# Recurrent gates as three products of split halves, with low parts made ahead, in a two-layer flow-matching step on one Trainium2 core

## The chip, the cores and the metric

The kernel runs on one core of one Trainium2 chip. The metric is the device time of one execution in microseconds (us). Before the change the median of three runs is 1498.4 us (1496.66 to 1498.74).

## The reference, cut to what matters

Two layers run over 512 latent and 128 context tokens of width 1024. Layer 0 mixes tokens by attention, layer 1 by a bidirectional gated linear recurrence; each is followed by a SwiGLU feed-forward of hidden width 2816, and each sub-layer is normed and modulated by vectors computed from a conditioning vector (`silu(cond) @ w_mod + b_mod`). What the change touches is the recurrence:

```python
gate, xr = jnp.split(xm @ w_in, 2, axis=-1)
xc = _centred_depthwise_conv(xr, conv_w, conv_b)
# for each direction, in 8 blocks of 128 channels:
r = jax.nn.sigmoid(jnp.einsum('btnk,nkj->btnj', xb, w_a) + b_a)
i = jax.nn.sigmoid(jnp.einsum('btnk,nkj->btnj', xb, w_i) + b_i)
log_a = -LRU_C * r * jax.nn.softplus(-lam)
a = jnp.exp(log_a)
b = jnp.sqrt(-jnp.expm1(2.0 * log_a)) * (i * xc)
h = a_t * h + b_t                      # scan over the tokens
y = (hs_f + hs_b) * jax.nn.gelu(gate)
return y @ w_out
```

So each block of 128 channels has four gate matrices of 128 x 128: two kinds (w_a, w_i) by two directions.

## The kernel before, in words

Activations lie with channels on the 128 partitions and tokens along the free axis; KT = 8 tiles of 128 channels, 640 tokens. Nearly all matrix products are done in a fast four-byte type (F32R) that rounds its operands. To keep the precision, every operand is split into a high part (a rounded copy) and a low part (the rest), and a product is three: high by high, high by low, low by high (`some`, L232 to 241). A weight is fetched by `unit` (L170): SP loads the raw weight (`raw`, three buffers), then either ScalarE copies it into the rounded type (L186) or, in phases whose only PSUM tag is "at" or where the call asks for it, POOL's queue loads it a second time with a cast (L184); VectorE subtracts to give the low part (L188). High and low parts have three buffers each (`whi`, `wlo`), with another set (`whx`, `wlx`) in some phases.

A weight unit of the feed-forward is eight k-tiles by three products by two chunks of tokens (322 and 320 columns: the first has two extra columns that carry the shift). `ffn` (L994) takes the hidden tiles in three groups of 8, 7 and 7: gate and up units of a group, then its down projection. In the first feed-forward five PSUM banks (three of `mm`, two of `mx`) take the chunks in turn, and VectorE and ScalarE empty them.

The modulation vectors are not matrix products on TensorE: they are sums on VectorE (`mod_cols`, L260), one 512 KB tile of w_mod at a time through POOL's queue into `mraw` (two buffers), with `mprod` (one buffer) for the product that nobody reads. They are written as a generator, 80 steps in all. `fill(n)` (L295) takes n steps of it out of a quota at set places in the program: after each weight unit's fetch and each down tile (FG = 1, 1, 1 says how many, for gate and up units and down tiles). `need` takes as many as it must.

The first feed-forward ends in `project_closing` (L657 on): the last down projection, the statistics and, in `normed`, the modulated norm of the recurrent layer's input, on VectorE and ScalarE in turns (L614 to 616), while TensorE already starts on the first input weights of the recurrent layer.

The recurrent layer goes over eight blocks f, software-pipelined by the loop at L1629: `lru_a(t)` convolves the block's input (one ScalarE step, L1395, and three on VectorE, L1397) and computes the four gate products (L1407) and their tanh (L1408); `lru_xr(t+1)` projects the next block's input; `lru_b(t-1)` makes a and b; `lru_c(t-2)` scans; `lru_gate` projects the gelu branch, `lru_d` multiplies and splits the output. Both projections take their weights through `halves` and `unit` (16 tiles of `wi`). The gate products are in single precision: gw (256 KB a block, loaded by SP, L1393) and xc are plain F32, the 643 columns (512 latent, 3 of padding, 128 context) are done as 512 and 131 in a two-bank PSUM tile `gp` with two buffers. The last block ends in `lru_end`, and `project_halves` goes on with the output weights (`wlo`), whose first parts of the product run before the last block is done (L1093, L1097).

The order of instructions on each engine is not the program's: a scheduler places them, by its own model of their times, with the program's order as priority; `pin` and `issue_after` add an order by hand. Each engine then runs its list in order.

Of the kernel before, what the change touches and what calls it, by code (L numbers as in the profile page):

```python
# [9 lines left out]
F32 = mybir.dt.float32  # L10
F32R = mybir.dt.float32r
AF = mybir.ActivationFunctionType
# [3 lines left out]
P = 128  # L16
# [15 lines left out]
EPS = 1e-6  # L32
NEG = -1e30
VW = 256
LW = 643
NLT = 10
C0 = 515
LATPR = (slice(0, 512), slice(C0, LW))
FG = (1, 1, 1)
MODS = ((0, 2), (0, 4), (0, 3), (0, 5), (1, 1), (1, 0), (1, 4), (1, 3), (1, 2), (1, 5))  # L40
NB = 2
KH = KT // 2
# [85 lines left out]
class _Step:  # L128
# [38 lines left out]
        self.read = self.nc.sync.dma_start(t, src).ins  # L167
        return t

    def unit(self, src, slot=None, after=None, nx=3, cast=False, raw=None):  # L170
        nc = self.nc
        _, a, b = src.shape
        raw = self.raw(src) if raw is None else raw
        if slot is None:
            self.nu += 1
            slot = "x" if self.wx and self.nu % 2 == 0 else "m"
        if slot == "x":
            hi, lo = self.wxs([P, a, b], nx)
        else:
            hi = self.t([P, a, b], F32R, "whi", 3)  # L180
            lo = self.t([P, a, b], F32R, "wlo", 3)
        if cast or self.ptags == ["at"]:
            with self.pin(self.cast if after else None):
                nc.gpsimd.dma_start(hi, src)  # L184
        else:
            nc.scalar.copy(hi, raw)  # L186
        with self.pin(after):
            self.low = nc.vector.tensor_tensor(lo, raw, hi.bitcast(F32), ALU.subtract).ins  # L188
        return hi, lo
# [96 lines left out]
    def modulations(self):  # L286
        yield from self.mod_gate(0, 2)
        yield from self.mod_ss(0, 3, 1)
        yield from self.mod_gate(0, 5)
        yield from self.mod_ss(1, 0, 0)  # L290
        yield from self.mod_ss(1, 3, 1)
        yield from self.mod_gate(1, 2)
        yield from self.mod_gate(1, 5)

    def fill(self, n):  # L295
        for _ in range(min(n, self.quota)):
# [697 lines left out]
    def ffn(self, l, hi, lo, fp, last):  # L994
        nc = self.nc
        f0 = 0
        for ci, n in enumerate((8, 7, 7)):
            hhi = self.big()
            hlo = self.big()
            sg = {}  # L1000

            def eg(j):
                def ev(t0, s, ps):
                    if t0:
                        sg[j] = self.t([P, NTOK], F32, "sg", 2, fp)
                    g = sg[j]
                    nc.vector.tensor_tensor(g[:, s], ps, self.rt[:, s], ALU.mult)
                    for c, a, b in _pieces(s.start, s.stop):
                        nc.scalar.activation(g[:, a:b], g[:, a:b], AF.Silu, bias=self.bias[:, c:c + 1])
                return ev  # L1010

            def eu(j):
                def ev(t0, s, ps):
                    u = self.t([P, 320], F32, "up", 2, fp)
                    nc.vector.tensor_tensor(u, ps, self.rt[:, s], ALU.mult)
                    for c, a, b in _pieces(s.start, s.stop):
                        g = sg[j][:, a:b]
                        nc.vector.scalar_tensor_tensor(g, u[:, a - t0:b - t0], self.bias[:, c:c + 1], g, ALU.add, ALU.mult)
                    self.split(hhi[:, j, s], hlo[:, j, s], sg[j][:, s])
                return ev  # L1020
            for j in range(n):
                f = f0 + j
                self.ws(self.i["gu"][l, f], hi, lo, eg(j), FG[0] * (f > 0), CHB)
                self.ws(self.i["gu"][l, NF + f], hi, lo, eu(j), FG[1] * (f > 0), CHB)
            w = self.i["dn"][l, :, :, f0:f0 + n]
            if ci == 2:
                last(w, hhi, hlo, (l, 5))
            else:
                self.project(w, hhi, hlo, (l, 5), done=lambda f: self.fill(FG[2]))
            f0 += n  # L1030
# [332 lines left out]
        c = CI["ba0"] * KT  # L1363
        nc.vector.tensor_scalar(self.hb, self.cols[:, c:c + 4 * KT], 0.5, None, ALU.mult)

    def halves(self, w, hi, lo, ev, after=None, slot=None):
        u = self.unit(w, slot, after, 2)
        return [lambda t0=t0, t1=t1, **kw: ev(t0, self.chunk(u, hi, lo, t0, t1, **kw)) for t0, t1 in CHL]

    def lru_xr(self, f, hi, lo, after=None):  # L1370
        xr = self.xrs[f % 2]
        nat = xr[:, 2:514].rearrange("p (r c) -> p c r", r=ROWS)

        def ev(t0, ps):
            for o, a, b, r in ((nat[:, 56:64], 0, 64, ROWS), (nat[:, 0:40], 64, 384, ROWS),
                               (nat[:, 40:56], 384, 512, ROWS), (xr[:, 517:645], 512, 640, 0)):
                if t0 <= a and b <= t0 + 384:
                    v = ps[:, a - t0:b - t0]
                    self.nc.scalar.copy(o, v.rearrange("p (c r) -> p c r", r=r) if r else v)
        return self.halves(self.i["wi"][KT + f], hi, lo, ev, after)  # L1380

    def turn(self, table, step):
        if table != self.table:
# [5 lines left out]

    def lru_a(self, f, lp):  # L1390
        nc, xr = self.nc, self.xrs[f % 2]
        gw = self.t([P, 2, 2, P], F32, "gw", 2, lp)
        nc.sync.dma_start(gw, self.i["wg"][f])  # L1393
        xc = self.t([P, LW], F32, "xc", 2, lp)
        nc.scalar.activation(xc, xr[:, 0:LW], AF.Identity, scale=self.col("cw0", f), bias=self.col("cb", f))  # L1395
        for j in range(1, 4):
            nc.vector.scalar_tensor_tensor(xc, xr[:, j:j + LW], self.col(f"cw{j}", f), xc, ALU.mult, ALU.add)  # L1397

        def lt():
            return self.t([P, 2, LW], F32, "lt", NLT, lp)  # L1400
        tr, ti = lt(), lt()
        for w, tl in enumerate((tr, ti)):
            for d in range(2):
                c = (w * 2 + d) * KT + f
                ps = self.pp.tile([P, 1024], F32, tag="gp", name=self.nm("gp"), bufs=2)
                for s0, s1 in ((0, 512), (512, LW)):
                    nc.tensor.matmul(ps[:, s0:s1], gw[:, w, d], xc[:, s0:s1], start=True, stop=True)  # L1407
                self.turn(AF.Exp, lambda: nc.scalar.activation(tl[:, d], ps[:, 0:LW], AF.Tanh, scale=0.5, bias=self.hb[:, c:c + 1]))  # L1408
        nc.vector.scalar_tensor_tensor(ti, ti, 1.0, xc[:, None, :].broadcast_to([P, 2, LW]), ALU.add, ALU.mult)
        return lt, tr, ti  # L1410

# [25 lines left out]
        return self.nc.vector.tensor_tensor(yv, fn[:, c0:c1], bn[:, c0:c1], ALU.add)  # L1437

    def states(self, f, h):
        ends = bass.AP(tensor=h.tensor, offset=h[:, 0, LW - 1:LW].offset, ap=[list(h.ap[0]), [C0 + 1, 2]])  # L1440
        return self.nc.vector.tensor_copy(self.st.rearrange("p (d k) -> p k d", d=2)[:, f], ends)

    def lru_c(self, f, a, h):
        for d in range(2):
            for part in range(2):
                self.scan(f, a, h, d, part)
        self.states(f, h)
        y = a[:, 0, 0:NTOK]
        for piece in ((56, 64, 0), (0, 56, 64)):
            self.directions(y, h, *piece)  # L1450
        self.nc.vector.tensor_tensor(y[:, NLAT:NTOK], h[:, 0, C0:LW], h[:, 1, C0:LW], ALU.add)
        return y

    def lru_d(self, f, y, G, yhi, ylo):
# [10 lines left out]
    def lru_end(self, f, a, h, root, G, yhi, ylo, late):  # L1465
# [28 lines left out]
        low(*CH[0])  # L1494
        dve(self.scan, f, a, h, 1, 1)
        dve(self.directions, y, h, 32, 56, 320)
        dve(nc.vector.tensor_tensor, y[:, NLAT:NTOK], h[:, 0, C0:LW], h[:, 1, C0:LW], ALU.add)
        gated(*CH[1])
        low(*CH[1])
        with self.pin(ins):  # L1500
# [9 lines left out]
    def lru_gate(self, f, hi, lo, lp, after=None):  # L1510
        nc = self.nc
        G = self.t([P, NTOK], F32, "gl", 3, lp)

        def ev(t0, ps):
            if t0 == 0 or f == KT - 1:
                nc.scalar.copy(G[:, t0:t0 + ps.shape[1]], ps)
            if t0 == 0:
                return
            for v, o in ((G, G),) if f == KT - 1 else ((ps, G[:, t0:NTOK]), (G[:, 0:t0], G[:, 0:t0])):
                self.turn(AF.Gelu_apprx_tanh, lambda: nc.scalar.activation(o, v, AF.Gelu_apprx_tanh))  # L1520
        return G, self.halves(self.i["wi"][f], hi, lo, ev, after)

    def new_x(self, st):
        pool = st.enter_context(self.tc.tile_pool(name="x", bufs=1, reuse_waits="tile"))
# [6 lines left out]
    def run(self):  # L1531
# [11 lines left out]
        nc.vector.memset(self.ones, 1.0)  # L1543
        self.st = self.t([P, 2 * KT], F32, "st", 1)
        self.cs = self.t([P, 2 * KT], F32, "cs", 1)
        dram = self.ctx.enter_context(tc.tile_pool(name="dram", bufs=1, space=bass.MemoryType.DRAM))
        mpool, xpool = ExitStack(), ExitStack()
        self.csb = self.t([P, 2, D], F32, "csb", 1, mpool.enter_context(tc.tile_pool(name="mods", bufs=1)))
        self.mask = self.t([P, 64], F32, "mask", 1)
# [46 lines left out]
        self.new_x(xpool)  # L1596
        self.load_x(i["x"])
        xd = dram.tile([D, NTOK], F32, tag="xd", name="xd")
        with self.phase("ffn0", at=2, rr=1, mx=2, wx=2, quota=56) as fp:
            self.project(i["wo"], ohi, olo, (0, 2), ((0, 1), xhi, xlo), None, True)  # L1600

            def last(w, hhi, hlo, gk):
                self.nh, self.nl = self.big(n=PITCH), self.big(n=PITCH)
                self.project_closing(w, hhi, hlo, gk, (1, 0), self.nh, self.nl, xd)
            self.ffn(0, xhi, xlo, fp, last)
        xpool.close()
        mpool.close()
        xhi, xlo = self.nh, self.nl
# [73 lines left out]
```

## Time and profile before

| | us |
|---|---|
| median of three runs | 1498.4 (1496.66 to 1498.74) |
| the profiled execution | 1496.74 |
| its span, first to last instruction | 1494.9 |
| TensorE busy | 1475.9 (99%) |
| VectorE busy | 1062.0 (71%) |
| ScalarE busy | 698.6 (47%) |
| POOL busy | 225.7 (15%) |

In the profile PE is TensorE, PEld its weight loads, DVE is VectorE, ACT is ScalarE, POOL is GpSimd and SP is SyncE, which issues most DMAs. L12 is line 12 of the kernel. A group's line gives line, engine, operation, output<-inputs by the program's names, shape and xcount, then the busy time in us and the mean of one in ns, then the idle time of the engine just before such instructions and what ended it. A timeline's line gives start and duration in us. A stretch's line gives its limits and length, then for each engine the busy time and number of instructions, the granted TensorE clock (1.00 is full), the DMA engines' share and GB/s. TensorE's products overlap one another by their pipeline, so what a product takes of the array is the distance from its start to the next start. "PE mm L239 <- ACT xr L1379: 0.5, 1, 0.5" says that line 239's product waited for that ScalarE step 0.5 us in total, once, 0.5 at the longest. A DMA line gives the issuing queue, the number of transfers, KB of each and the median us from issue to landing.

### The profile page before, as it was taken

The page shows a single profiled execution, that of the slowest core. Times are in us where ns is not written, and L with a number is a line of the kernel's source. Part 1 is how long each engine was busy: PE and PEld are TensorE (multiplying, and loading weights), DVE is VectorE, ACT ScalarE, POOL GpSimd, SP SyncE. Part 2 cuts the span into 40 slices and gives each one's busy share as a digit, 9 for nine tenths or more (in the row PEclk, how much of TensorE's full clock was granted, in tenths as well). Part 3 has the DMA queues.
Part 4 walks back from the last instruction along what each step waited for, and adds up shares of the span by engine and source line. Part 5 has one row for each costly group of instructions (what it writes and reads, how often), then busy time and mean ns, then how long its engine had stood idle before and what let it go on. Part 6 is the DMA issues. An engine that isn't in the chain of part 4 may idle for free. (4 is left out here: it accounts for less than half of the span.)

```text
span 1494.9 us, 26171 instructions
## 1 busy us (share of the span) xinstructions
PE 1475.9 (99%) x10399; PEld 1433.0 (96%) x10399; DVE 1062.0 (71%) x2019; ACT 698.6 (47%) x1269; POOL 225.7 (15%) x264
## 2 busy tenths in 40 slices
PE   9999999999999999999999999999999999999997
PEld 7999999899999999999999988899999999999997
DVE  5778998679999987444443769886975666655645
ACT  5676667754332123312321569875634343424243
POOL 0212132101111110000000100000331322232311
PEclk9999999999999999999999999999999999999999
DMA  9645665345566664222222444335333131313111
GB/s 378 201 128 177 196 189 163 105 156 183 196 187 195 207 197 142 63 85 85 66 62 96 142 145 126 115 115 194 102 130 98 57 114 57 113 57 111 59 57 71
DMA packets 73050, 198.88 MB, mean 133 GB/s; under 512 B 8128, under 2 KB 24672, under 8 KB 72800
## 3 DMA queue, kind: packets, MB, share of 16 engines
q1 hardware_dynamic: 57360, 142.31, 29.9%
q0 software_dynamic: 14960, 54.21, 11.8%
q8 instruction: 82, 1.34, 0.4%
q10 hardware_dynamic: 608, 0.69, 0.1%
q14 instruction: 40, 0.33, 0.1%
HBM read 181.05 MB, written 8.92 MB: 127 GB/s over the span
## 5 line engine op out<-in xcount | busy, mean ns | idle before, releaser
L240 PE MATMUL mm<-big,whi 128*128 128x320 f32 (+3 forms) x1193 | 371.2, 311 | 0.8 <-DVE big L1508 0.6
L239 PE MATMUL mm<-big,whi 128*128 128x320 f32 (+3 forms) x1193 | 369.0, 311 | 1.6 <-ACT big L615 0.6
L241 PE MATMUL mm<-big,wlo 128*128 128x320 f32 (+3 forms) x1193 | 368.8, 310 | 0.0
L239 PEld LDWEIGHTS mm<-big,whi 128*128 128x128 f32 x1193 | 223.9, 188 | 3.7 <-ACT big L615 0.9
L240 PEld LDWEIGHTS mm<-big,whi 128*128 128x128 f32 x1193 | 224.2, 188 | 2.8 <-DVE big L1508 1.0
L241 PEld LDWEIGHTS mm<-big,wlo 128*128 128x128 f32 x1193 | 224.7, 188 | 1.1
L268 DVE SCALAR_TENSOR_TENSOR mprod<-mraw,csb 128x1024 f32<-128x1024 f32 x160 | 194.8, 1218 | 11.3 <-DMA mraw<-in_wm 10.8
L639 DVE SCALAR_TENSOR_TENSOR x<-mm,G,x 128x128 f32<-128x128 f32 (+3 forms) x193 | 77.4, 433 | 78.5 <-PE mm L241 77.0
L186 ACT CAST whi<-raw 128x1024 fp32r<-128x1024 f32 (+1 forms) x70 | 72.8, 1040 | 106.1 <-PE mm L240 71.2
L188 DVE TENSOR_TENSOR wlo<-raw,whi 128x1024 fp32r<-128x1024 f32 (+1 forms) x87 | 105.1, 1208 | 23.9 <-ACT whi L186 11.0
L240 PE MATMUL mm<-big,whx 128*128 128x320 f32 (+3 forms) x363 | 112.2, 309 | 0.0
L241 PE MATMUL mm<-big,wlx 128*128 128x320 f32 (+3 forms) x363 | 112.1, 309 | 0.0
L239 PE MATMUL mm<-big,whx 128*128 128x320 f32 (+3 forms) x363 | 111.9, 308 | 0.0
L264 POOL DMA_DIRECT2D mraw<-in_wm x80 | 43.4, 543 | 355.5 <-DVE mprod L268 257.3
L240 PE MATMUL mx<-big,whi 128*128 128x320 f32 (+3 forms) x299 | 92.1, 308 | 0.0
L239 PE MATMUL mx<-big,whi 128*128 128x320 f32 (+3 forms) x299 | 91.9, 307 | 0.0
L241 PE MATMUL mx<-big,wlo 128*128 128x320 f32 (+3 forms) x299 | 91.8, 307 | 0.0
L186 ACT CAST whx<-raw 128x1024 fp32r<-128x1024 f32 (+1 forms) x38 | 39.1, 1028 | 94.1 <-PE mm L240 54.5
L1506 ACT CAST whi<-raw 128x1024 fp32r<-128x1024 f32 (+1 forms) x41 | 41.3, 1007 | 69.0 <-PE mm L240 43.0
L240 PE MATMUL mx<-big,whx 128*128 128x320 f32 (+3 forms) x234 | 72.9, 312 | 0.0
L241 PE MATMUL mx<-big,wlx 128*128 128x320 f32 (+3 forms) x234 | 72.6, 310 | 0.0
L239 PE MATMUL mx<-big,whx 128*128 128x320 f32 (+3 forms) x234 | 72.4, 309 | 0.0
(409 smaller groups left out, 3734.3 us busy)
## 6 DMA issues: line engine op xcount, KB each, us to landing
raw<-in_gu SPq DMA_DIRECT2D x88, 512.0 KB, 3.5
mraw<-in_wm POOLq DMA_DIRECT2D x80, 512.0 KB, 3.9
raw<-in_dn SPq DMA_DIRECT2D x24, 512.0 KB, 3.6
sw<-in_wm SPq DMA_DIRECT2D x16, 512.0 KB, 10.2
raw<-in_wqk SPq DMA_DIRECT2D x16, 512.0 KB, 4.9
raw<-in_wi SPq DMA_DIRECT2D x16, 512.0 KB, 3.5
whi<-in_wi POOLq DMA_DIRECT2D x16, 512.0 KB, 3.8
raw<-in_dn SPq DMA_DIRECT2D x16, 448.0 KB, 3.3
```

The lines of the kernel that those rows point to most:

```text
L186: nc.scalar.copy(hi, raw)
L188: self.low = nc.vector.tensor_tensor(lo, raw, hi.bitcast(F32), ALU.subtract).ins
L239: nc.tensor.matmul(ps, hi[:, k], xhi[:, k, s], start=(k == 0), stop=False)
L240: nc.tensor.matmul(ps, hi[:, k], xlo[:, k, s], start=False, stop=False)
L241: self.done = nc.tensor.matmul(ps, lo[:, k], xhi[:, k, s], start=False, stop=(k == last)).ins
L264: nc.gpsimd.dma_start(w, self.i["wm"][l * 6 + j - 2, f])
L268: nc.vector.scalar_tensor_tensor(prod, w, 1.0, self.csb[:, s], ALU.mult, ALU.mult, accum_out=out[:, s, f:f + 1])
L639: self.added = self.nc.vector.scalar_tensor_tensor(xs, ps[:, a - t0:b - t0], G[:, s, f:f + 1], xs, ALU.mult, ALU.add).ins
L1506: self.nc.scalar.copy(hi, v)
```

## The change

Three things change.

The gate products are made like all others: gw is loaded in the rounded type by POOL's queue (a cast on the way), its low part comes from DRAM by SP, and xc is split into xh and xl (ScalarE's copy, VectorE's subtraction). The two live in the buffers of the tag `raw`. The width becomes 644, two halves of 322 columns, one in each bank of `gp`, with three products for each: six F32R products of 322 columns for each gate in place of single-precision ones of 512 and 131.

The low parts of the sixteen input weights and the eight tiles of gate weights are no longer made in the recurrent layer. A new generator, `lows`, is put behind the modulations: for each tile it loads the weight twice on POOL's queue (plain into `mraw`, with the cast into `mprod`), subtracts on VectorE, and stores the low part to DRAM on POOL's queue. In the recurrent layer SP loads the low part into `wlo`; the raw load and VectorE's subtraction are gone, the cast load of the high part on POOL's queue stays.

To make room for the 24 steps, the quota of the first feed-forward goes from 56 to 80, and gate and up units of its third group take three steps each instead of one.

```diff
-LW = 643
+LW = 644
+LE = 643
-FG = (1, 1, 1)
+FG = (1, 3, 1)
...
+        if low is None:
+            raw = self.raw(src) if raw is None else raw
...
+        if low is not None:
+            nc.sync.dma_start(lo.bitcast(F32), low)
+            return hi, lo
         with self.pin(after):
             self.low = nc.vector.tensor_tensor(lo, raw, hi.bitcast(F32), ALU.subtract).ins
...
+    def lows(self):
+        nc = self.nc
+        for key, src in self.split_ahead:
+            shape = list(src.shape)
+            raw = self.t(shape, F32R, "mraw", 2, self.sb)
+            nc.gpsimd.dma_start(raw.bitcast(F32), src)
+            hi = self.t(shape, F32R, "mprod", 1, self.sb)
+            nc.gpsimd.dma_start(hi, src)
+            nc.vector.tensor_tensor(raw, raw.bitcast(F32), hi.bitcast(F32), ALU.subtract)
+            self.low_parts[key] = self.dram.tile(shape, F32, tag=f"low{key[0]}{key[1]}", name=f"low{key[0]}{key[1]}")
+            nc.gpsimd.dma_start(self.low_parts[key], raw.bitcast(F32))
+            yield
...
-                self.ws(self.i["gu"][l, f], hi, lo, eg(j), FG[0] * (f > 0), CHB)
-                self.ws(self.i["gu"][l, NF + f], hi, lo, eu(j), FG[1] * (f > 0), CHB)
+                self.ws(self.i["gu"][l, f], hi, lo, eg(j), FG[ci > 1] * (f > 0), CHB)
+                self.ws(self.i["gu"][l, NF + f], hi, lo, eu(j), FG[ci > 1] * (f > 0), CHB)
...
-    def halves(self, w, hi, lo, ev, after=None, slot=None):
-        u = self.unit(w, slot, after, 2)
+    def halves(self, k, hi, lo, ev, after=None):
+        u = self.unit(self.i["wi"][k], None, after, 2, low=self.low_parts["i", k])
...
-        gw = self.t([P, 2, 2, P], F32, "gw", 2, lp)
-        nc.sync.dma_start(gw, self.i["wg"][f])
+        gw, gl = [self.t([P, 2, 2, P], F32R, v, 2, lp) for v in ("gw", "gx")]
+        nc.gpsimd.dma_start(gw, self.i["wg"][f])
+        nc.sync.dma_start(gl.bitcast(F32), self.low_parts["g", f])
...
+        xh, xl = [self.t([P, D], F32R, "raw", 3)[:, 0:LW] for j in range(2)]
+        self.split(xh, xl, xc)
...
-                for s0, s1 in ((0, 512), (512, LW)):
-                    nc.tensor.matmul(ps[:, s0:s1], gw[:, w, d], xc[:, s0:s1], start=True, stop=True)
-                self.turn(AF.Exp, lambda: nc.scalar.activation(tl[:, d], ps[:, 0:LW], AF.Tanh, scale=0.5, bias=self.hb[:, c:c + 1]))
+                gs = ps.rearrange("p (b c) -> p b c", b=2)[:, :, 0:LW // 2]
+                for v, x in ((gw, xh), (gl, xh), (gw, xl)):
+                    for b in range(2):
+                        nc.tensor.matmul(gs[:, b], v[:, w, d], x[:, b * LW // 2:(b + 1) * LW // 2], start=(x is xh and v is gw), stop=(x is xl))
+                o = tl[:, d].rearrange("p (b c) -> p b c", b=2)
+                self.turn(AF.Exp, lambda: nc.scalar.activation(o, gs, AF.Tanh, scale=0.5, bias=self.hb[:, c:c + 1]))
...
-        with self.phase("ffn0", at=2, rr=1, mx=2, wx=2, quota=56) as fp:
+        with self.phase("ffn0", at=2, rr=1, mx=2, wx=2, quota=80) as fp:
...
+            assert next(self.mods, None) is None
```

The order of the 24 tiles (`split_ahead`) is that in which the recurrent layer needs its input weights, then the gate weights. The remaining lines of the change replace LW by LE where the last of 643 columns is meant.

More of the change, by code (lines that the diff above doesn't have):

```diff
@@ L34 @@
 VW = 256
-LW = 643
+LW = 644
+LE = 643
 NLT = 10
 C0 = 515
-LATPR = (slice(0, 512), slice(C0, LW))
-FG = (1, 1, 1)
+LATPR = (slice(0, 512), slice(C0, LE))
+FG = (1, 3, 1)
 MODS = ((0, 2), (0, 4), (0, 3), (0, 5), (1, 1), (1, 0), (1, 4), (1, 3), (1, 2), (1, 5))
@@ L168, in raw, with unit @@
         return t
-    def unit(self, src, slot=None, after=None, nx=3, cast=False, raw=None):
+    def unit(self, src, slot=None, after=None, nx=3, cast=False, raw=None, low=None):
         nc = self.nc
         _, a, b = src.shape
-        raw = self.raw(src) if raw is None else raw
+        if low is None:
+            raw = self.raw(src) if raw is None else raw
         if slot is None:
@@ L293, in modulations @@
         yield from self.mod_gate(1, 5)
+        yield from self.lows()
+    def lows(self):
[10 more added lines that the diff above has]
+            yield
     def fill(self, n):
@@ L1379, in ev @@
                     self.nc.scalar.copy(o, v.rearrange("p (c r) -> p c r", r=r) if r else v)
-        return self.halves(self.i["wi"][KT + f], hi, lo, ev, after)
+        return self.halves(KT + f, hi, lo, ev, after)
     def turn(self, table, step):
@@ L1439, in states @@
     def states(self, f, h):
-        ends = bass.AP(tensor=h.tensor, offset=h[:, 0, LW - 1:LW].offset, ap=[list(h.ap[0]), [C0 + 1, 2]])
+        ends = bass.AP(tensor=h.tensor, offset=h[:, 0, LE - 1:LE].offset, ap=[list(h.ap[0]), [LW + C0 - LE + 1, 2]])
         return self.nc.vector.tensor_copy(self.st.rearrange("p (d k) -> p k d", d=2)[:, f], ends)
@@ L1450, in lru_c @@
             self.directions(y, h, *piece)
-        self.nc.vector.tensor_tensor(y[:, NLAT:NTOK], h[:, 0, C0:LW], h[:, 1, C0:LW], ALU.add)
+        self.nc.vector.tensor_tensor(y[:, NLAT:NTOK], h[:, 0, C0:LE], h[:, 1, C0:LE], ALU.add)
         return y
@@ L1496, in lru_end @@
         dve(self.directions, y, h, 32, 56, 320)
-        dve(nc.vector.tensor_tensor, y[:, NLAT:NTOK], h[:, 0, C0:LW], h[:, 1, C0:LW], ALU.add)
+        dve(nc.vector.tensor_tensor, y[:, NLAT:NTOK], h[:, 0, C0:LE], h[:, 1, C0:LE], ALU.add)
         gated(*CH[1])
@@ L1520, in ev @@
                 self.turn(AF.Gelu_apprx_tanh, lambda: nc.scalar.activation(o, v, AF.Gelu_apprx_tanh))
-        return G, self.halves(self.i["wi"][f], hi, lo, ev, after)
+        return G, self.halves(f, hi, lo, ev, after)
     def new_x(self, st):
@@ L1545, in run @@
         self.cs = self.t([P, 2 * KT], F32, "cs", 1)
-        dram = self.ctx.enter_context(tc.tile_pool(name="dram", bufs=1, space=bass.MemoryType.DRAM))
+        self.dram = dram = self.ctx.enter_context(tc.tile_pool(name="dram", bufs=1, space=bass.MemoryType.DRAM))
+        self.low_parts = {}
+        order = [KT, 0, KT + 1] + [k for f in range(1, KT) for k in ((f, KT + f + 1) if f + 1 < KT else (f,))]
+        self.split_ahead = [(("i", k), i["wi"][k]) for k in order] + [(("g", f), i["wg"][f]) for f in range(KT)]
         mpool, xpool = ExitStack(), ExitStack()
```

## The prediction

> **What bounds the kernel now.** I read the page's shares first, then the busy time in stretches around the places that the change touches, and then what TensorE waited for there.
>
> ```profile
> PE 1475.9 (99%) x10399; PEld 1433.0 (96%) x10399; DVE 1062.0 (71%) x2019; ACT 698.6 (47%) x1269; POOL 225.7 (15%) x264
> PEclk9999999999999999999999999999999999999999
> ```
> ```profile
> core 0: us, PE busy (x) PEld busy (x) DVE busy (x) ACT busy (x) POOL busy (x), PEclk, DMA share, GB/s
> 578.00:815.00 237.00, 237.00 (x1591) 237.00 (x1590) 103.42 (x183) 64.02 (x120) 0.55 (x1) 1.00 0.26 79
> 815.00:850.00 35.00, 33.57 (x243) 32.27 (x241) 26.84 (x72) 13.12 (x33) 3.50 (x11) 1.00 0.39 119
> 850.00:980.00 130.00, 129.41 (x785) 113.77 (x785) 105.45 (x127) 103.48 (x145) 6.91 (x13) 1.00 0.42 126
> 980.00:1010.00 30.00, 28.50 (x197) 28.23 (x196) 25.85 (x36) 20.11 (x25) 2.67 (x5) 1.00 0.43 138
> ```
> TensorE is busy from end to end at a granted clock of 1.00, so time goes only where TensorE gets less work or fewer waits; whatever VectorE, ScalarE or the queues gain or lose counts only where it reaches TensorE. The stretches are: the rest of the first feed-forward (578 to 815), its closing norm (815 to 850), the recurrent layer (850 to 980), the handover to the second feed-forward (980 to 1010). In the feed-forward TensorE has no gap at all and VectorE is idle 134 us of 237. In the recurrent layer VectorE (81%) and ScalarE (80%) are both near TensorE. The waits of TensorE from 815 to 1010:
>
> ```profile
> PE mm L1093 <- ACT big L1481: 1.5, 1, 1.5
> PE at L592 <- DVE ssq L578: 0.7, 1, 0.7
> PE mm L239 <- ACT big L615: 0.6, 1, 0.6
> PE mm L239 <- ACT xr L1379: 0.5, 1, 0.5
> PE mm L240 <- DVE big L616: 0.2, 1, 0.2
> ```
> That is all there is to win besides the work itself: 2.0 us in the closing norm (the last four rows), 1.5 us at the handover (the first).
>
> **The gate products.** One gate of one block is two single-precision matmuls, of 512 and 131 columns; the profile has two records for each (128 records for 32 gates), and draws the four together:
>
> ```profile
> 877.59 0.28 PE L241 MATMUL mm<-big,wlo 128*128 128x256 f32 x1
> 877.71 1.25 PE L1407 MATMUL gp<-xc,gw 128*128 128x512 f32 x4
> 878.70 0.36 PE L239 MATMUL mm<-big,whi 128*128 128x256 f32 x1
> 878.91 0.28 PE L240 MATMUL mm<-big,whi 128*128 128x256 f32 x1
> 879.03 0.28 PE L241 MATMUL mm<-big,wlo 128*128 128x256 f32 x1
> ```
> The durations overlap, so I count from start to start. A 256-column product moves on every 0.12 us. The gate holds the array from 877.71 to 878.70, 0.99 us, and the product behind it needs 0.21 instead of 0.12, so a gate costs 1.08 us and 32 of them 34.6 us. After the change a gate is six products of 322 columns of the split type. That shape runs in the first feed-forward:
>
> ```profile
> 600.00 0.31 PE L240 MATMUL mm<-big,whi 128*128 128x322 f32 x1
> ...
> 601.17 0.31 PE L239 MATMUL mm<-big,whi 128*128 128x322 f32 x1
> ```
> There are eight starts from the first row to the second, 1.17 us, so 0.147 us each; six make 0.88. TensorE loses 0.20 us a gate: 32 x 0.20 = **6.4 us less work**. With single starts read as 0.145 or 0.150 it is 6.7 or 5.8. The Trainium skill, page "TensorE: Matmul & The Clock Gate", section "Back-to-back issue gap", gives N / 2.4 + 2.5 ns for an isolated product at full clock, which is 137 ns for 322 columns, and an estimate from that page would take 8.3 us off instead of 6.4. The trace has 147 ns for this very shape in this kernel's stream, so the trace decides.
>
> **What the gates need first.** Splitting xc adds, for each of eight blocks, a ScalarE copy and a VectorE subtraction of 644 columns; the nearest rows are those of the outputs' 640 columns. Taken away are the VectorE subtractions of the sixteen input weights:
>
> ```profile
> L1508 DVE TENSOR_TENSOR big<-lt,big 128x640 fp32r<-128x640 f32 x5 | 4.1, 826 | 0.0
> L1506 ACT CAST big<-lt 128x640 fp32r<-128x640 f32 x5 | 3.7, 738 | 0.4 <-DVE lt L1455 0.4
> ```
> ```profile
> L188 DVE TENSOR_TENSOR wlo<-raw,whi 128x1024 fp32r<-128x1024 f32 x18 | 22.0, 1223 | 12.9 <-DMA whi<-in_wi 6.5 <-issue 4.6 <-PE gp L1407 1.9
> ```
> VectorE: plus 8 x 0.83 = 6.6, minus 16 x 1.22 = 19.5 (two of the 18 are of the next weights), so 13 us less, and its 6.5 us of waiting for the cast transfers go too. ScalarE: plus 8 x 0.74 = 5.9 us. In 850 to 980 that makes ScalarE 109 of some 124 us, 88%, VectorE about 75%. The conv-to-gate path becomes 1.6 us longer per block. I cost this at nothing inside the layer, because TensorE has a whole input projection (two units of 24 products per chunk) to do between blocks, and ScalarE now waits for the gates and not the other way round:
>
> ```profile
> L1408 ACT ACTIVATE lt<-gp,l_hb 128x643 f32<-128x643 f32 x32 | 24.9, 797 | 19.6 <-PE gp L1407 19.4
> ```
> If that cover is gone, the ScalarE copies cost at most their 5.9 us (a rival, below). A gain here is excluded: TensorE is busy 129.41 of 130.
>
> **The closing norm.** Three of the removed subtractions lie in the stretch in which VectorE feeds the norm:
>
> ```profile
> 827.00 1.22 DVE L188 TENSOR_TENSOR wlo<-raw,whi 128x1024 fp32r<-128x1024 f32 x1 [1.45 <-DMA whi<-in_wi]
> ...
> 835.97 1.21 DVE L188 TENSOR_TENSOR wlo<-raw,whi 128x1024 fp32r<-128x1024 f32 x1
> ...
> 840.32 1.22 DVE L188 TENSOR_TENSOR wlo<-raw,whi 128x1024 fp32r<-128x1024 f32 x1
> ```
> ```profile
> 827.00:850.00 23.00, 21.57 (x143) 20.27 (x141) 22.91 (x61) 11.35 (x29) 2.03 (x9) 1.00 0.42 133
> ```
> Behind the first, VectorE is hardly idle until the norm is done, so it comes 1.2, 2.4 and 3.65 us earlier in turn. The four waits there are 0.7, 0.6 + 0.2 and 0.5, each shorter than what VectorE has gained by then (the one for xr is ScalarE's, queued behind the norm that VectorE paces). I take **2.0 us** off. The bounds: 0, if the low parts land late or ScalarE sets the pace, and 2.8 with TensorE's slower restarts. What moves here are queue entries: the low part's transfer stands in SP's queue where the raw weight's stood, but waits for a buffer that TensorE frees, as the cast on POOL does; behind it on SP are stores of x, which nobody awaits before the handover. The casts start and land so:
>
> ```profile
> 822.85 0.59 POOL L184 DMA_DIRECT2D whi<-in_wi  x1 [0.61 <-PE mm L241]
> ```
> ```profile
> raw<-in_wi SPq DMA_DIRECT2D x16, 512.0 KB, 3.5
> whi<-in_wi POOLq DMA_DIRECT2D x16, 512.0 KB, 3.8
> gw<-in_wg SPq DMA_DIRECT2D x8, 256.0 KB, 2.9
> mraw<-in_wm POOLq DMA_DIRECT2D x80, 512.0 KB, 3.9
> ```
> A low part of 512 KB lands beside its cast, and earlier than cast plus subtraction did.
>
> **Low parts in the feed-forward.** 24 items (16 of 512 KB, 8 of 256 KB), each two loads and a store on POOL's queue and one subtraction. They follow the modulations, whose last load and the transfer behind it stand here:
>
> ```profile
> 570.87 0.54 POOL L264 DMA_DIRECT2D mraw<-in_wm  x1 [5.20 <-DVE mprod L268]
> 578.31 0.55 POOL L184 DMA_DIRECT2D whx<-in_wlo  x1 [6.90 <-DVE mprod L268]
> ```
> The second is a weight of the layer after next, loaded as soon as its memory is free: queues are filled far ahead of program order, so the low parts should start near 575, whatever the fills of 1, 1 and 3 say. The buffer for the rounded part is single, so an item is issue, landing, subtraction: 0.54 + 3.9 + 1.22 = 5.7 us; the small ones 0.54 + 2.9 + 0.65 (half of 1.22, an estimate) = 4.1. 16 x 5.7 + 8 x 4.1 = 124 us, done near 700, 120 us before POOL's first cast for the recurrent layer. VectorE's work there rises from 103 to 128 of 237 us. Cost to TensorE: 0, hidden by VectorE's idle time and five PSUM banks of one 3.5 us chunk each (24 x 0.147). A gain is excluded (237.00 of 237), the loss is the second rival. The gate weights' cast moves from SP to POOL and lands a block ahead: 0.
>
> **The handover.** From 962 on ScalarE has no slack:
>
> ```profile
> 962.00:998.00 36.00, 36.00 (x234) 33.60 (x233) 32.62 (x39) 35.19 (x43) 2.12 (x4) 1.00 0.30 90
> ```
> In the last block it has one more copy (0.74 us) and TensorE's cover is four gates shorter (4 x 0.20 = 0.8). So the 1.5 us wait for the last output grows by **1.5 us**. xh and xl also take two of the three buffers through which the output weights are read, so the second and third of these come only after the last gate. Bounds: 0 (VectorE's relief carries it) to 6 (a 3.6 us landing, a cast and a subtraction, all late).
>
> **Sum.** 6.4 + 2.0 - 1.5 = 6.9 us less. The profiled execution took 1496.74 us (span 1494.9): 1489.8. The median of the runs shown is 1.7 above that execution, so 1498.4 - 6.9 = **1491.5 us**.
>
> **Rivals.**
> *ScalarE binds.* It evacuates every PSUM tile of the layer; if its added 5.9 us all reach TensorE, the gain is 8.4 - 1.5 - 5.9 = 1.0 us: 1497.4, no change that can be seen. For: 35.19 of 36 at the end. Against: its 19.4 us of waiting for gates.
>
> *VectorE held in the feed-forward (slower).* A subtraction that waits for its cast holds all evacuations behind it. VectorE has 44% of its time taken, so of a weight unit's 7.1 us of TensorE 4.0 are free. An item held through its landing takes 5.7, so one in each unit overdraws by 1.7; 24 of them make 41 us, less the 14 us that four free banks cover: +27, in all near 1518. It decides as soon as items wait on VectorE in a row rather than other work being placed between. For: VectorE's 6.5 us of waits on casts above show that it does get held. The Trainium skill's page "TensorE: Matmul & The Clock Gate", section "Architectural detail: the array is 16× 32×32, not 1× 128×128", says VectorE takes its instructions strictly in order, by which nothing passes a held one; the trace agrees so far as those waits go. Against: 16 casts cost 6.5 us there, 0.4 each, not 3.9.
>
> *All waits go.* Norm 2.8 and handover 1.5 vanish as well: 6.4 + 4.3 = 10.7, 1487.7.
>
> *The products don't get the fast rate.* Then 3 x 644 columns at 1.08 us per 643 is 3.25 us a gate, 32 x 2.17 = 69 us more, near 1560. Against: the 322-column row.
>
> **Chances.** Forecast 0.63, all waits go 0.09, ScalarE binds 0.18, VectorE held 0.07, slow rate 0.03. About 0.2% (3 us) is what a measurement of this kernel can tell from no change. The first two are faster by more: 0.72; the third is within: 0.18; the last two slower: 0.10. The range goes from the case without waits, widened by the 6.7 us bound of the gates, 1487, to the ScalarE case with 2 us for a late weight, 1499.5; it leaves out the two slow cases and a little at either end.
>
> **What would show it.** Right: 192 products of 322 columns at the gates' line, 0.147 apart, no record of 512 and 131; the four waits of the norm gone; 24 subtractions between 575 and 720 with TensorE gapless; the wait for the last output at 2 to 4 us. Wrong: TensorE idle from 578 to 815 behind VectorE; waits for xl, for a low part, or for ScalarE's evacuations between 850 and 980; a wait for output weights at the handover above 4 us.

## The result, and the profile after

The changed kernel takes 1506.28 us (median of four runs, 1504.71 to 1510.96) against 1497.63 us before: the ratio is 1.0063, with a 95% interval of 1.0051 to 1.0075. It is slower by about 9 us, where 6.9 us less had been forecast. The profiled execution has a span of 1502.9 us. Line numbers in it are 1 to 25 higher than before.

The page of the changed kernel, engine totals:

```profile
PE 1473.5 (98%) x10463; PEld 1443.6 (96%) x10463; DVE 1069.8 (71%) x2035; ACT 700.2 (47%) x1277; POOL 269.1 (18%) x344
```
TensorE is busy 2.4 us less than before, in a span that is 8 us longer: it has less work and more waits. The waits after the low parts begin, first in the feed-forward (590 to 830), then around the handover (980 to 1050):

```profile
PE mm L244 <- DVE up L1034: 3.4, 2, 1.7
PE mm L245 <- DVE big L1533: 1.6, 1, 1.6
PE mm L244 <- ACT big L1531: 1.5, 1, 1.5
PE mm L244 <- DVE x L658: 1.0, 1, 1.0
PE mx L244 <- DVE sg L1026: 0.7, 1, 0.7
```
```profile
PE mm L1112 <- ACT big L1506: 2.1, 1, 2.1
PE at L611 <- DVE ssq L597: 1.2, 1, 1.2
PE mx L246 <- DVE wlo L193: 1.1, 1, 1.1
PE mm L1135 <- DVE wlo L193: 0.5, 1, 0.5
```
In the feed-forward, where TensorE had no wait at all, it now waits for VectorE to empty PSUM banks (`up`, `sg`, `x`) or for the hidden tiles (`big`), which VectorE and ScalarE make. These are six stops of 8.2 us in all. Of the closing norm's four waits one is left in the list from 830 to 990, and it is shorter:

```profile
PE mm L244 <- ACT gl L1545: 0.4, 1, 0.4
PE gp L1431 <- ACT lt L1433: 0.4, 1, 0.4
PE mm L244 <- ACT xr L1398: 0.3, 1, 0.3
```

To see where time goes, I number TensorE's products without the gates' own (10,271 in either trace), count each start from the first product's, and subtract the start of the same number in the kernel before. What this shift grows by in a stretch is what the stretch lost or won:

| stretch (products) | before, us | after: shift grows by |
|---|---|---|
| start to the first feed-forward (to 4500) | 0 to 602 | +1.0 |
| first feed-forward (4500 to 6000) | 602 to 824 | +10.3 |
| closing norm (6000 to 6150) | 824 to 847 | -2.2 |
| recurrent layer (6150 to 6800) | 847 to 975 | -5.2 |
| handover (6800 to 7200) | 975 to 1036 | +4.8 |
| the rest (7200 to the last) | 1036 to 1487 | 0.0 |

The 1.0 at the start is there within the first 200 products and was anything from 0.0 to 1.2 in the runs below, so it belongs to the execution and not to the change. The feed-forward's 10.3 are more than the 8.2 us of waits because starts are counted here: a wait is counted from the end that the profile gives the product ahead, about 0.16 us behind where the next one would have started, and the second start behind a stop comes 0.1 us late (0.25 us behind the first at 735.88, where others come 0.147 apart); a seventh, short stop of some 0.3 us is in no row of the list. The border between layer and handover is uncertain by about 1 us, as the order of products there differs between kernels.

The gates themselves do what was worked out. Two gates, twelve products:

```profile
965.97 0.46 PE L1431 MATMUL gp<-raw,gw 128*128 128x322 f32 x2
966.27 0.47 PE L1431 MATMUL gp<-raw,gx 128*128 128x322 f32 x2
966.57 0.76 PE L1431 MATMUL gp<-raw,gw 128*128 128x322 f32 x4
967.16 0.46 PE L1431 MATMUL gp<-raw,gx 128*128 128x322 f32 x2
967.46 0.46 PE L1431 MATMUL gp<-raw,gw 128*128 128x322 f32 x2
967.75 0.34 PE L246 MATMUL mm<-big,wlo 128*128 128x384 f32 x1
967.93 0.34 PE L244 MATMUL mm<-big,whi 128*128 128x384 f32 x1
```
From 965.97 to 967.75 is 1.78 us, 0.89 a gate, against 1.08 before. All 32 gates took 28.8 us from start to start, with a few short waits among them, against 34.6: 5.8 us less.

What holds VectorE in the feed-forward is in its own waits there, the first three of 578 to 815:

```profile
DVE mraw L309 <- DMA mprod<-in_wi: 40.5, 13, 5.2
DVE mraw L309 <- DMA mprod<-in_wg: 21.9, 6, 5.6
DVE mraw L309 <- issue: 13.0, 4, 4.9
```
Line 309 is the low part's subtraction. It waits 75 us in all, up to 5.6 at a time; 62 of them, in 19 of 23 waits, are for the cast load. One such wait on VectorE's timeline, and what TensorE did behind it:

```profile
726.99 0.48 DVE L1034 TENSOR_TENSOR up<-mx,r 128x320 f32<-128x320 f32 x1
733.12 0.69 DVE L309 TENSOR_TENSOR mraw<-mraw,mprod 128x512 fp32r<-128x512 f32 x1 [5.65 <-DMA mprod<-in_wg]
733.73 0.68 DVE L1037 SCALAR_TENSOR_TENSOR sg<-up,bias,sg 128x192 f32<-128x192 f32 x2
...
735.34 0.48 DVE L1034 TENSOR_TENSOR up<-mm,r 128x320 f32<-128x320 f32 x1
```
```profile
735.88 0.42 PE L244 MATMUL mm<-big,whx 128*128 128x322 f32 x1 [1.64 <-DVE up L1034]
```
The row at 726.99 empties a bank. Then nothing runs on VectorE until the cast load lands, and the step at 733.73 runs behind it, although its inputs were ready when 726.99 was done (ScalarE's share in them ended at 726.6). The next bank is emptied at 735.34 only, and TensorE has stood for 1.64 us by then. All seven stops of TensorE in the feed-forward come like this, with a waiting subtraction ahead of the step that releases them; for the one that waits for `big` from ScalarE, ScalarE itself had waited 5.18 us for VectorE. The last of the 24 subtractions starts at 749, where the prediction had them done near 700. And the cast loads land later than modulation tiles of the same size did:

```profile
mraw<-in_wm POOLq DMA_DIRECT2D x80, 512.0 KB, 3.9
mprod<-in_wi POOLq DMA_DIRECT2D x16, 512.0 KB, 5.7
```

### The profile page after: what moved, and what is told of

The parts are those of the page before. It is cut to its first block, busy times and chain, and to the rows that moved or that the text cites. A ratio compares the mean times of both kernels' runs of the same rounds, so it can differ in the third digit from the quotient of the medians.

```text
span 1502.9 us, 26463 instructions
## 1 busy us (share of the span) xinstructions
PE 1473.5 (98%) x10463; PEld 1443.6 (96%) x10463; DVE 1069.8 (71%) x2035; ACT 700.2 (47%) x1277; POOL 269.1 (18%) x344
## 5 line engine op out<-in xcount | busy, mean ns | idle before, releaser
L193 DVE TENSOR_TENSOR wlo<-raw,whi 128x1024 fp32r<-128x1024 f32 (+1 forms) x71 | 85.6, 1206 | 11.9 <-ACT whi L188 11.8
L309 DVE TENSOR_TENSOR mraw<-mraw,mprod 128x1024 fp32r<-128x1024 f32 (+1 forms) x24 | 25.1, 1048 | 75.4 <-DMA mprod<-in_wi 40.5
L244 PEld LDWEIGHTS mm<-big,whx 128*128 128x128 f32 x363 | 68.4, 188 | 4.9 <-DVE up L1034 1.9
L245 PE MATMUL mx<-big,whx 128*128 128x320 f32 (+3 forms) x234 | 72.9, 312 | 0.0
```

What stands on the lines that cost most here:

```text
L244: nc.tensor.matmul(ps, hi[:, k], xhi[:, k, s], start=(k == 0), stop=False)
L245: nc.tensor.matmul(ps, hi[:, k], xlo[:, k, s], start=False, stop=False)
```

## The experiments

The theory: each subtraction stands on VectorE's list ahead of work that is ready, waits for a load that lands late, and holds that work; TensorE runs out of free banks. The rivals: the 30 MB of added transfers crowd out the weights' own loads; VectorE simply has too much to do; or the gates' new operands are at fault.

**Low parts alone.** The changed kernel with the gates of the kernel before:

```diff
-        xh, xl = [self.t([P, D], F32R, "raw", 3)[:, 0:LW] for j in range(2)]
-        self.split(xh, xl, xc)
...
-                for v, x in ((gw, xh), (gl, xh), (gw, xl)):
-                    for b in range(2):
-                        nc.tensor.matmul(gs[:, b], v[:, w, d], x[:, b * LW // 2:(b + 1) * LW // 2], start=(x is xh and v is gw), stop=(x is xl))
+                for s0, s1 in ((0, 512), (512, LE)):
+                    nc.tensor.matmul(ps[:, s0:s1], gw[:, w, d], xc[:, s0:s1], start=True, stop=True)
```


> The low parts are made in the first feed-forward and the input weights' ones are used, but the gates stay in single precision with 643 columns (the gate weights' low parts are made and not used). Theory (VectorE, held by each low part's subtraction until the cast load lands, keeps TensorE's PSUM banks from being emptied): TensorE comes out of the first feed-forward 8 to 12 us later than in the kernel before, gets 2 to 3 back in the closing norm, and neither gains nor loses over 1 in the recurrent layer and the handover: near 1505. Rival (the split gates or their memory cause the loss): the feed-forward loses under 2 and the kernel is near 1496.

It took 1504.74 us (before, on the same chip: 1497.92). TensorE's shift grew by 11.9 in the feed-forward, fell by 2.2 in the closing norm and by 0.4 in the recurrent layer and 0.7 in the handover. So the whole loss in the feed-forward, and the whole gain in the closing norm, belong to the low parts, and the layer's 5 us and the handover's loss to the split gates.

**Transfers without subtractions.**

```diff
-            nc.vector.tensor_tensor(raw, raw.bitcast(F32), hi.bitcast(F32), ALU.subtract)
```


> The changed kernel without the 24 subtractions in the first feed-forward: all loads, cast loads and stores of the low parts stay, so what is stored as a low part is the plain weight. Theory (VectorE held): TensorE has no gap between 578 and 815, so the kernel is 10 us faster than the changed one, near 1496. Rival (the transfers crowd the weights' own loads): the feed-forward still loses about 10, near 1506.

1494.41 us. TensorE busy in the feed-forward, here and in the next experiment, after the line of the changed kernel (the columns are those of the stretches in the prediction):

```profile
578.00:815.00 237.00, 228.77 (x1533) 226.82 (x1532) 120.43 (x201) 60.31 (x118) 38.78 (x72) 1.00 0.61 203
```
```profile
578.00:815.00 237.00, 237.00 (x1592) 237.00 (x1591) 104.28 (x183) 64.67 (x121) 39.14 (x72) 1.00 0.62 205
```
The DMA engines are as full as in the changed kernel (0.62 against 0.61, 205 GB/s against 203), and TensorE has no gap. Crowding is ruled out as a cause by itself.

**Subtractions without waiting.**

```diff
+        raw = self.t([P, KT, P], F32R, "mraw", 2, self.sb)
+        nc.gpsimd.dma_start(raw.bitcast(F32), self.i["wi"][KT])
...
-            nc.gpsimd.dma_start(hi, src)
-            nc.vector.tensor_tensor(raw, raw.bitcast(F32), hi.bitcast(F32), ALU.subtract)
+            nc.vector.tensor_tensor(hi[:, 0:m], raw[:, 0:m].bitcast(F32), raw[:, 0:m].bitcast(F32), ALU.subtract)
```


> The changed kernel with the 24 subtractions of the same size, but all of one tile that was loaded once, so none waits for a load; the stores stay, and what is stored is no low part. Theory (VectorE held): no loss in the feed-forward, near 1496, although VectorE has the same 25 us more of work there. Rival (VectorE's added work itself): TensorE still loses 10 us there, near 1506.

1494.77 us:

```profile
578.00:815.00 237.00, 237.00 (x1592) 237.00 (x1591) 126.93 (x208) 65.00 (x121) 13.37 (x25) 1.00 0.35 119
```
VectorE is busier than in the changed kernel (126.93 against 120.43), and TensorE again has no gap. The work isn't the cause either. This run does without the loads as well (DMA share 0.35), so only the two runs together tell: neither half alone costs anything, and the loss needs a subtraction that waits for a load.

**Two buffers for the rounded part.**

```diff
-            hi = self.t(shape, F32R, "mprod", 1, self.sb)
+            hi = self.t(shape, F32R, "mprod" if len(self.low_parts) % 2 else "lhi", 1, self.sb)
```


> The changed kernel with two buffers for the rounded part in turns instead of one, so that an item's cast load can be issued before the item ahead is subtracted; the subtractions stay on VectorE. If the hold comes from the single buffer: VectorE's waits for the cast loads fall from 75 us to under 30 and TensorE's loss in the feed-forward from 10 us to under 3, near 1498. If the hold comes from where the schedule puts the subtraction (too early for the real landing): the waits stay over 50 us and the loss over 6.

1497.78 us; the feed-forward lost 4.7. Neither pair of numbers came out as a pair: the waits for the cast loads fell to 1.2 us and the time is near 1498, as by the first reading, but the loss stayed above 3. VectorE's waits were mostly these:

```profile
DVE mraw L309 <- DMA mraw<-in_wi: 34.8, 6, 8.7
DVE mraw L309 <- DMA mraw<-in_wg: 19.6, 6, 5.5
DVE mraw L309 <- issue: 7.7, 2, 5.1
```
That is still 62 us, but now in 14 waits instead of 23, and for the plain load: with the cast load issued ahead, the two buffers of `mraw`, each of which must first be stored, came last (GpSimd's queue waits 35 us for such stores before it issues a plain load). A second buffer moved the wait to the next scarce buffer and halved the loss. TensorE's loss isn't in proportion to the waits, as only some of them end in a stop of TensorE: three here, seven in the changed kernel. Whether the places that the schedule gives the subtractions have a share of their own stays open.

**Subtractions on GpSimd.**

```diff
-            nc.vector.tensor_tensor(raw, raw.bitcast(F32), hi.bitcast(F32), ALU.subtract)
+            nc.gpsimd.tensor_tensor(raw, raw.bitcast(F32), hi.bitcast(F32), ALU.subtract)
```


> The changed kernel with the 24 subtractions of low parts on GpSimd instead of VectorE; everything else, the transfers too, is as it was. Theory (VectorE held by them): TensorE has no gap between 578 and 815, the 10 us come back, and the closing norm, the recurrent layer and the handover stay as in the changed kernel: 1495 to 1497. If GpSimd's subtractions get in VectorE's way at SBUF: a loss of 2 or more stays in the feed-forward.

1494.96 us, no loss in the feed-forward; closing norm -2.2, recurrent layer -5.3, handover +4.7. The same loads are waited for, 50 us in all, but on an engine behind which nothing of the feed-forward stands.

**xl in a buffer of its own.**

```diff
-        xh, xl = [self.t([P, D], F32R, "raw", 3)[:, 0:LW] for j in range(2)]
+        xh, xl = self.t([P, D], F32R, "raw", 3)[:, 0:LW], self.t([P, LW], F32R, "xl", 1, lp)
```


> The changed kernel with xl in a buffer of its own, so that only xh passes through the three buffers by which the output weights are read. If those buffers cause the handover's loss: the second output weight is read some 10 us earlier, TensorE's 1.1 us wait for its low part goes, and the 4.8 us lost between the recurrent layer's end and the second feed-forward become 3 or less: 1503 to 1505. If the last block's chain on ScalarE causes it: 4.8 as before, near 1506. The loss in the first feed-forward stays at 10.

1502.79 us. SP's loads of the output weights, in the kernel before, the changed one and this one:

```profile
946.86 34.58 SPq L167 DMA_DIRECT2D raw<-in_wlo  x6
```
```profile
968.00 22.98 SPq L168 DMA_DIRECT2D raw<-in_wlo  x6
```
```profile
963.26 24.39 SPq L168 DMA_DIRECT2D raw<-in_wlo  x6
```
The loads start earlier by 5 us, not by 10. TensorE's waits for the low parts of output weights (1.1 and 0.5) and for the next norm's statistics (`ssq`, 1.2) are gone; in return it waits 0.9 more for ScalarE's evacuation (`gl`) just ahead of the handover. From the closing norm's end to product 7200 layer and handover together give 2.3 us back (4.35 won, 2.05 lost) where the changed kernel gets 0.4 (5.24 and 4.82), so the shared buffers cost 1.9 us. The feed-forward lost 10.4 as before.

**The split gates alone.** Low parts made where they are needed, the feed-forward untouched; for want of memory xh, xl and gl have one buffer each:

```diff
-        yield from self.lows()
...
+        gr = self.t([P, 2, 2, P], F32, "raw", 3)
+        nc.sync.dma_start(gr, self.i["wg"][f])
+        nc.vector.tensor_tensor(gl, gr, gw.bitcast(F32), ALU.subtract)
...
+        xh, xl = [self.t([P, LW], F32R, v, 1, lp) for v in ("xh", "xl")]
```


> Only the split gates: the input weights' low parts are made on VectorE in the recurrent layer and the closing norm as in the kernel before, the gate weights' low parts on VectorE in the recurrent layer, nothing is added to the feed-forward; xh and xl have one buffer each. By the terms of the changed kernel's trace: 0 in the feed-forward, 0 in the closing norm, and in the recurrent layer and handover together between a gain of 5 (the gates' products alone decide) and 0 (ScalarE and VectorE, now with both the old and the new work, decide): 1493 to 1498.

1502.70 us, worse than the range that I gave. The feed-forward and the norm neither lost nor won (0.0 and +0.1), but layer and handover together lost 5.9:

```profile
PE mm L1107 <- ACT big L1503: 3.4, 1, 3.4
PE mm L240 <- ACT gl L1542: 1.7, 2, 0.9
PE gp L1428 <- DVE xl L1530: 1.4, 1, 1.4
PE mm L1107 <- DMA big<-lt: 1.3, 1, 1.3
```
TensorE waits for the last output, for ScalarE's evacuations, and for xl itself; further ahead, from 850 to 950, it also waits 2.7 us for ScalarE's xr. With the old subtractions still on VectorE, the six microseconds of the gates are more than used up. So the split gates don't pay without the low parts made ahead, in this form; the single buffers may have a share in it that this run doesn't separate.

**Both mends**, GpSimd's subtractions and xl's buffer:

> The changed kernel with both mends: subtractions of low parts on GpSimd, xl in a buffer of its own. If the two losses are independent: 1506 less 10 less 2, so 1493 to 1495.5, faster than the kernel before by 0.15 to 0.35%.

1493.14 us (seven runs, 1491.61 to 1493.79) against 1497.16: the ratio is 0.9970, interval 0.9959 to 0.9981. The gain is the sum of the two, as the first case had it, and with both losses mended the change as a whole is worth having. How much of that is the gates' was not run by itself: outside the feed-forward the run with low parts alone won 3.4 us up to product 7200 (2.25, 0.40 and 0.72), and this one 5.1, so an estimate for the split gates is 1.7 us. What is left at the handover is a loss of 1.4 us, and the wait for the last output is now 2.4.

**Less on ScalarE.** Three runs asked whether ScalarE sets that wait, each with both mends: the copy for xh moved to VectorE, the copies for two output weights replaced by cast loads, and both.

```diff
-        self.split(xh, xl, xc)
+        nc.vector.tensor_copy(xh, xc)
+        nc.vector.tensor_tensor(xl, xc, xh.bitcast(F32), ALU.subtract)
```


> The kernel with both mends (subtractions of low parts on GpSimd, xl in its own buffer), and the rounded copy of xc made on VectorE instead of ScalarE. If ScalarE's work sets the time from the last gates to the last output: its chain is 0.7 to 1.5 us shorter, and the wait for the last output falls from 2.4 to between 1 and 1.7, so the handover loses 1 less than with both mends: near 1492. If VectorE sets it: 2.4 or more as before, 1493 to 1494.

```diff
-        us = [self.unit(w[f], "mmx"[f], cast=f == 2) for f in range(3)]
+        us = [self.unit(w[f], "mmx"[f], cast=True) for f in range(3)]
```


> The kernel with both mends, and the rounded copies of the first two output weights made by a cast load on POOL's queue instead of by ScalarE, 2.1 us of ScalarE's work in its full stretch. If ScalarE's work sets the last output: the wait for it falls from 2.4 to under 1 and the handover's loss of 2.5 to about 0.5, near 1491. If VectorE's work after ScalarE's last root sets it: 2.4 stays, 1493.

> Both at once: the rounded copy of xc on VectorE, and the first two output weights' rounded copies by cast loads. If ScalarE's work sets the last output: the wait goes altogether and the kernel is 2 to 3 us faster than with the two mends, 1490 to 1491.5; if VectorE's does, no faster than 1493.

They took 1492.63 us, 1490.61 us (one run each) and 1490.55 us (five runs, 1489.30 to 1491.22, against 1497.10: ratio 0.9953, interval 0.9939 to 0.9966). The waits for the last output, in the second and the third:

```profile
PE mm L1112 <- ACT big L1506: 2.7, 1, 2.7
```
```profile
PE mm L1112 <- ACT big L1507: 1.6, 1, 1.6
```
The copy of xc alone did not help: the wait for the last output stayed at 2.4, a wait of 1.2 us for the next norm's statistics on VectorE came back, and layer and handover together won 1.9 us against 2.9 with the two mends. The casts did not shorten the wait for the last output either: it rose to 2.7, and is 1.6 with both. The price of ScalarE's load near the end stays open between two readings. By the shift, layer and handover improve by 0.2 us with the casts and by 0.7 with both (3.1 and 3.5 won). The times improve by 2.5 (a single run) and 2.6 (medians, with intervals that just overlap); in the profiled executions the gain is 1.9 and 1.4, and what of that lies outside layer and handover is in stretches that moved by up to 1.2 us from run to run without a change there. What sets the last output itself is not settled either. The last version has the lowest median of all, 0.47% below the kernel before.

## Why the prediction was wrong, point by point

The gates' products were right: 0.88 us a gate worked out, 0.89 measured in the gates shown; all of them gave 5.8 of the 6.4. The layer won 5.2: TensorE lost 0.6 at the wait for gl, 0.3 of the gates' gain lies behind the layer's border, and 0.3 was won at the wait for xr, which the prediction had counted with the closing norm. The closing norm was right: 2.0 forecast with that wait, 2.2 measured without it. The runs with low parts alone (2.2 won) and with split gates alone (nothing won) show that it comes from no longer making the low parts there.

The step that failed is "Cost to TensorE: 0, hidden by VectorE's idle time and five PSUM banks": the runs showed a cost of 10.3 us there. Forecast and measurement lie 15.6 us apart on TensorE's own count: 10.3 by this step, 3.3 at the handover, 1.2 in the layer and 1.0 at the start, less 0.2 in the closing norm. The start near 575 was right (the first load was issued at 575.27), and so was VectorE's added work. But idle time in the sum of a stretch is not idle time at the moment of an instruction. VectorE's list is fixed, and a subtraction that waits takes the idle time in a lump, with the evacuations behind it. Two numbers under that step were off. An item's landing was taken as 3.9 us from the modulations' loads, and was 5.7 with two loads and a store of each item under way. And the price of a hold was taken from the casts in the recurrent layer, 0.4 us each; here VectorE's waits were 75 us over 24, 3.1 each.

The mechanism itself was on record as the rival "VectorE held", with a chance of 0.07 and +27 us. Its sign and place were right, its size was too large by more than two: 10.3. It had every item hold VectorE for 5.7 us, subtraction included, against 4.0 free; the mean was 3.1 of waiting and 1.0 of subtraction, which by that sum would have been covered by the free banks. TensorE was stopped all the same, seven times, and not by the longest holds: the seven waits of 3.5 to 5.2 us that end from 650 to 701, during a down projection, stopped it once, the seven of 1.6 to 5.65 us from 709 to 750, during gate and up units, four times. So the length of a hold alone doesn't decide; that it is what VectorE has to empty behind it fits these two stretches, but no run shows it by itself. The row that spoke for it, VectorE's 6.5 us on casts, was read as reassuring because the mean was small. The casts are not issued earlier there: 3.8 to 7.5 us ahead of the subtraction, against 3.0 to 6.8 here. But there VectorE mostly had other work placed in between, and 5 of 16 subtractions waited for the cast; here 19 of 24 did. The Trainium skill's page "TensorE: Matmul & The Clock Gate", section "Architectural detail: the array is 16× 32×32, not 1× 128×128", has VectorE strictly in order; the trace agrees, by the 5.65 us wait in front of a step that was ready. The rival deserved more than 0.07.

The handover had the right sign, but neither its size nor its step: 1.5 forecast, with 6 as the bound, and 4.8 measured. The wait for the last output, on which the 1.5 rested, grew from 1.5 to 2.1 us only. The jumps of the shift put the rest elsewhere: 1.3 and 0.6 us where TensorE waits for low parts of output weights, 1.4 where it waits for the next norm's statistics, 0.3 at the last gate, and 0.6 at the last output; some 0.6 are spread. The output weights that wait for the buffers of xh and xl were named there and left out of the value; for the statistics the prediction has no term. With xl in its own buffer the two waits for low parts and the one for the statistics are gone, for 1.9 us net.

The rival "ScalarE binds" at its full price didn't come: the layer kept its 5 us. "All waits go" didn't either.

## What to carry to other kernels

Work put into an engine's idle time is free only if it never waits there: ask of each added instruction what it waits for, when that can be issued at the earliest given its buffers, and what stands behind it on the same engine. If it must wait, put it on an engine that nobody needs in that stretch, or give every buffer in its loop a second copy, not just one (a second copy of one halved the loss here; of all, it was not run). And when a scarce buffer is lent to a new user, look for who next reads through it.

## What the runs showed of the hardware

GpSimd's subtractions made VectorE's slower where they met. VectorE's subtraction for the hidden tiles, between 578 and 700, in the kernel before and with the low parts on GpSimd, and GpSimd's own:

```profile
L1508 DVE TENSOR_TENSOR big<-sg,big 128x320 fp32r<-128x320 f32 x12 | 5.8, 487 | 2.6 <-ACT big L1506 2.6
```
```profile
L1533 DVE TENSOR_TENSOR big<-sg,big 128x320 fp32r<-128x320 f32 x12 | 12.3, 1030 | 2.6 <-ACT big L1531 2.6
```
```profile
L309 POOL TENSOR_TENSOR mraw<-mraw,mprod x24: 1282/2396/3257, 583.4 to 774.8; 128x1024 fp32r<-128x1024 f32 x16, 128x512 fp32r<-128x512 f32 x8
```
Its mean goes from 487 to 1030 ns, but the mean hides what happens: nine of the twelve take 0.48 to 0.49 us as before, and three take 2.6 to 2.7. Each of these three meets a subtraction on GpSimd and ends 0.35 to 0.36 us behind it; none of the nine meets one. One of the three:

```profile
618.13 2.40 POOL L309 TENSOR_TENSOR mraw<-mraw,mprod 128x1024 fp32r<-128x1024 f32 x1 [1.51 <-DMA mprod<-in_wi]
```
```profile
618.31 2.58 DVE L1533 TENSOR_TENSOR big<-sg,big 128x320 fp32r<-128x320 f32 x1 [0.53 <-ACT big L1531]
```
So VectorE's instruction stands while GpSimd's runs. The Trainium skill's page "SBUF — State Buffer", section "Who interferes with whom", says that a VectorE instruction with two inputs in SBUF contends with a GpSimd one that reads SBUF; these rows agree. It cost TensorE nothing here (237.00 of 237 busy): these holds of some 2 us were covered, as were 16 of VectorE's 23 waits in the changed kernel.

The products of split halves also leave no restart behind them. The product behind a single-precision gate, or a pair of them, moved on 0.08 to 0.09 us late in all 26 places; behind the split ones it was on time to within 0.01 us in all 23 (967.75 to 967.93 above, as between others of 384 columns).
